# Layer 1 starts its queries and keys on half of the width, with its opening loads in another order

## The chip, the core and the metric

One core of a Trainium2 chip runs the kernel. The time is that of the device, in microseconds (us), from the first to the last instruction of one execution and what lies around it. Five engines work in parallel, each through its own list of instructions in order: PE (matmul; PEld is its weight load), DVE and POOL (elementwise), ACT (activations, and a queue of DMAs), SP (only DMAs).

## The reference

Two layers of a hybrid transformer run over 512 latent tokens (x) and 256 context tokens (ctx), width 1024, in fp32. The change touches the first lines of a layer: modulation, norm, and the queries and keys of the neighbourhood attention.

```python
mod = (jax.nn.silu(c) @ mod_w[i] + mod_b[i])[:, None, :]
mod_c = (jax.nn.silu(c_ctx) @ mod_w[i] + mod_b[i])[None, None, :]
sh_m, sc_m, g_m, sh_f, sc_f, g_f = jnp.split(mod, 6, axis=-1)
csh_m, csc_m, cg_m, csh_f, csc_f, cg_f = jnp.split(mod_c, 6, axis=-1)
h = rms_norm(x, norm_attn_w[i]) * (1.0 + sc_m) + sh_m
hc = rms_norm(cx, norm_attn_w[i]) * (1.0 + csc_m) + csh_m
ua, ub, ug = jnp.split(h @ w_in[i], splits, axis=-1)
uca, ucb, ucg = jnp.split(hc @ w_in[i], splits, axis=-1)
ya, yca = neighbourhood_attention(ua, uca, na_rpb[i], ctx_out)
yb, ycb = ssd_mixer(ub, ucb, ...)
yg, ycg = gqa_attention(ug, ucg, ...)
x = x + g_m * (jnp.concatenate([ya, yb, yg], axis=-1) @ w_out[i])
# then a SwiGLU with sh_f, sc_f, g_f, the same for ctx in layer 1 only, and a last rms_norm
```

## The kernel before

The width of 1024 is cut into eight slices of 128 (d or k = 0 to 7) on the partitions; a row of a tile is a slice over 768 tokens, 512 of x and 256 of ctx. An fp32 product is made of three matmuls of rounded parts (high by high, low by high, high by low). load_w (L332) loads a weight block of 128x1024 into wr, ACT copies the high part into wh (L336), and DVE takes the low part wl as the difference (L337). make_h (L314) makes the normed and modulated activations: a multiply by the token scale and by the modulation scale on DVE or ACT and POOL (L324 to L327), the high part by ACT with the shift as bias (L329), the low part by DVE (L330). The high parts are HY for d 0 to 3 and HS for d 4 to 7, the low parts HZ and PHA, PHB.

The modulation of a layer has 12 chunks of 512 columns. In layer 1 chunk 0 and 1 are the two halves of the shift, 2 and 3 those of the scale; one half serves d 0 to 3, the other d 4 to 7. mod_chunk (L187) computes one on PE from eight loads of 256 KB (L179): eight matmuls with 32 columns of weights (L189), a copy to SBUF on DVE (L196), small transposing matmuls (L199), the sum with the bias (L201) and, for a scale, L265. Chunks 4 to 9 are made aside while the projections run: mod_rows (L207) loads the two conditioning vectors as rows (in_cvec, through the MA and MB buffers, L213) and takes their SiLU (L214 to L216), and mod_dots multiplies rows of the transposed weights by them on POOL (L239), sums on ACT (L240) and ends in two adds on DVE (L248, L250). The program's generator md spreads these over the stages.

The opening loads x by token blocks, then chunks 0 and 2, ctx, and chunks 1 and 3 (SP queue); blocks 0 and 1 of w_blk (queries of the neighbourhood attention) come behind. With all four chunks and both scales there, make_h runs for x and ctx, and the 192 matmuls of blocks 0 and 1 (L348) run over d = 0 to 7. spill (L541, on ACT's DMA queue) sends the queries to DRAM through MA and MB, two buffers each. Then come blocks 2 and 3 (keys, each spilled as it is done), the weights of the grouped attention's keys and values (w_kvdt, L362), and blocks 4 and 5 (values, transposed at L595). S is a PSUM tile of 128x1024, of which there are two; PT and sm are half as large, two each. Later stages of layer 1, in order: head_out with the rotary step on DVE (L678 on POOL, L694 and L697 on DVE), the convolution (L771), the remaining projections, attention (scores L400) and the state-space chunks, whose decay row goes through DRAM (crow, L876 and L901). skip (L937) multiplies on POOL.

A scheduler orders the instructions of each engine from the code's priorities and a simulated timeline; so what a diff moves in the code is not what moves on each engine.

## Time and profile before

| what | value |
|---|---|
| median of three runs | 1828.59 us |
| lowest and highest | 1812.85 and 1829.15 us |
| the profiled execution | 1826.39 us |
| its span, first to last instruction | 1824.6 us |
| mean granted clock of TensorE | 0.976 |
| busy of the span: PE, PEld, DVE, ACT, POOL | 95%, 81%, 58%, 37%, 22% |
| HBM traffic | 121 GB/s over the span |

The profile is of one execution. Times in it are from the start of the span. A line of a timeline gives start and duration of a run of like instructions, and in brackets how long the engine sat idle before it and what ended that.

### The profile page before, as it was taken

What the parts mean: (1) busy time and instruction counts of PE and PEld (TensorE: products, weight loads), DVE (VectorE), ACT (ScalarE), POOL (GpSimd) and SP (SyncE); (2) the same over time, 40 slices, a digit from 0 to 9 for tenths busy, and PEclk for the clock granted to TensorE, in tenths of its full rate; (3) what the DMA queues carried; (4) which work ended last, traced back from release to release, by engine and by line L of the source; (5) the groups of instructions that cost most, each with busy time, mean ns of one, the idle gap of its engine ahead of it and who ended that gap; (6) DMA issues with size and microseconds to landing.
All of it is one profiled execution on the core that took longest, in us unless ns stands there. A gap on an engine that the chain in (4) does not pass through costs nothing.

```text
span 1824.6 us, 26613 instructions
## 1 busy us (share of the span) xinstructions
PE 1735.0 (95%) x10146; PEld 1477.7 (81%) x10146; DVE 1056.2 (58%) x2165; ACT 683.9 (37%) x1376; POOL 401.6 (22%) x429
## 2 busy tenths in 40 slices
...
GB/s 364 186 152 123 194 144 182 122 89 66 73 61 135 119 116 117 114 103 118 115 127 115 120 157 189 81 114 112 150 74 65 98 93 93 104 94 94 102 106 79
DMA packets 94319, 221.66 MB, mean 121 GB/s; under 512 B 18416, under 2 KB 26224, under 8 KB 94192
## 3 DMA queue, kind: packets, MB, share of 16 engines
...
q14 instruction: 47, 0.39, 0.1%
HBM read 198.49 MB, written 21.43 MB: 121 GB/s over the span
## 4 chain that ended last, share of the span: by engine, by line
PE 78%; DVE 8%; DMA 6%; ACT 3%; issue 3%; POOL 2%; SPq 0%; ACTq 0%; DVEq 0%; POOLq 0%
PE S L348 60%; DMA wl<-crow 3%; PE sm L446 3%; PE PT L362 2%; PE sm L362 2%; PE PT L434 2%; DMA wr<-in_mod_wT_dram 1%; PE S L400 1%; PE PT L348 1%; PE sm L930 1%; PE sm L931 1%; PE PT L975 1%; PE S L189 1%; PE S L403 1%; DVE wl L337 1%
## 5 line engine op out<-in xcount | busy, mean ns | idle before, releaser
L336 ACT ACTIVATE wh<-wr 128x1024 fp32r<-128x1024 f32 (+3 forms) x204 | 197.9, 971 | 721.0 <-PE S L348 534.7
L337 DVE TENSOR_TENSOR wl<-wr,wh 128x1024 fp32r<-128x1024 f32 (+3 forms) x204 | 231.0, 1133 | 176.1 <-ACT wh L336 173.8
L280 POOL TENSOR_TENSOR tiny<-tiny,mhalf 128x2 f32<-128x2 f32 (+2 forms) x17 | 28.7, 1689 | 1068.3 <-DVE tiny L1181 1019.8
L348 PE MATMUL S<-HY,wh 128*128 128x512 f32 (+1 forms) x716 | 217.0, 361 | 8.8 <-DVE MB L294 4.5
L348 PE MATMUL S<-HZ,wh 128*128 128x512 f32 (+1 forms) x716 | 213.8, 356 | 0.6 <-DVE HZ L330 0.6
L348 PE MATMUL S<-HY,wl 128*128 128x512 f32 (+1 forms) x716 | 212.1, 354 | 0.7 <-DVE wl L337 0.7
L348 PE MATMUL S<-HS,wh 128*128 128x512 f32 (+1 forms) x716 | 212.3, 354 | 0.0
L348 PE MATMUL S<-HS,wl 128*128 128x512 f32 (+1 forms) x716 | 209.1, 350 | 0.0
L242 DVE CUSTOM_DVE_ANT_0 PT<-wr,XFB 128x512 f32<-128x512 f32 x112 | 75.6, 716 | 185.8 <-DMA wr<-in_mod_wT_dram 185.8
L348 PEld LDWEIGHTS S<-HY,wh 128*128 128x128 f32 x716 | 119.4, 192 | 27.3 <-issue 4.7
L348 PEld LDWEIGHTS S<-HZ,wh 128*128 128x128 f32 x716 | 120.0, 192 | 22.4 <-DVE HZ L330 2.1
L348 PEld LDWEIGHTS S<-HY,wl 128*128 128x128 f32 x716 | 118.3, 191 | 20.1 <-DVE wl L337 1.0
L348 PEld LDWEIGHTS S<-HS,wh 128*128 128x128 f32 x716 | 117.2, 189 | 18.2
L348 PEld LDWEIGHTS S<-HS,wl 128*128 128x128 f32 x716 | 116.2, 188 | 18.9
L348 PE MATMUL S<-PHA,wh 128*128 128x512 f32 (+1 forms) x358 | 105.8, 352 | 0.0
L348 PE MATMUL S<-PHB,wh 128*128 128x512 f32 (+1 forms) x358 | 104.6, 350 | 0.0
L348 PE MATMUL S<-GX,wh 128*128 128x512 f32 (+1 forms) x400 | 97.7, 350 | 0.4 <-DVE KA L1135 0.4
L425 POOL TENSOR_SCALAR pr<-pr,tiny 128x640 f32<-128x640 f32 (+2 forms) x80 | 68.1, 854 | 99.7 <-DVE tiny L424 78.6
L434 PE MATMUL PT<-c,pr 128*128 128x128 f32 x384 | 67.2, 292 | 11.1 <-ACT PHA L438 3.6
L1282 DVE TENSOR_TENSOR MB<-S,MA 128x768 f32<-128x768 f32 (+1 forms) x42 | 34.6, 824 | 70.5 <-PE S L348 70.5
L239 POOL TENSOR_TENSOR KA<-QN,XFB 128x512 f32<-128x512 f32 x48 | 67.1, 1404 | 36.9 <-ACT XFB L216 24.5
L348 PEld LDWEIGHTS S<-GX,wh 128*128 128x128 f32 x400 | 65.9, 189 | 11.2 <-DVE KA L1135 0.8
...
## 6 DMA issues: line engine op xcount, KB each, us to landing
...
```

The lines of the kernel that those rows point to most:

```text
L189: PE.matmul(pm[32 * j : 32 * j + 32, 0:512], lhsT=cs[:, k, :], rhs=w[k], start=(k < 4), stop=(k >= 4), tile_position=(0, 32 * j),)
L239: G.tensor_tensor(out=p_, in0=wv, in1=x, op=ALU.mult)
L242: V.tensor_tensor_reduce(out=p_, in0=wv, in1=x, scale=1.0, scalar=0.0, op0=ALU.mult, op1=ALU.add, accum_out=acc[:, o : o + 1],)
L280: POW.tensor_tensor(out=y, in0=v, in1=mhalf[:, 0:n], op=ALU.pow)
L336: S.activation(hi, raw, AF.Copy)
L337: V.tensor_tensor(lo, raw, hi.bitcast(F32), ALU.subtract)
L348: ins = PE.matmul(pt[:, c0:c1], lhsT=w, rhs=xx[:, c0:c1], start=(k == (0 if len(order) == 1 else order[0]) and i == 0), stop=(k == (nk - 1 ...
L362: PE.matmul(pt[:, 0:n], lhsT=s, rhs=w[:, o : o + n], start=(k == 0 and i == 0), stop=(k == KB - 1 and i == 2),)
L425: G.tensor_scalar(out=p_, in0=p_, scalar1=m[:, 4:5], scalar2=1.0, op0=ALU.mult, op1=ALU.mult)
L434: PE.transpose(pt[:, k * P : (k + 1) * P], pr[j, qi][:, kk * P : (kk + 1) * P], ident)
L446: PE.matmul(pv[64 * j : 64 * j + 64, 0:P], lhsT=V2(kts[k], j), rhs=ph[j, qi][:, k, :], start=(k == 0), stop=(k == nkt - 1), tile_position= ...
L1282: V.tensor_tensor(gg[:, c0:c1], pu[:, c0:c1], sg[:, c0:c1], ALU.mult)
```

## The change

The opening of layer 1 is written anew. All of x is loaded first (half of it into other buffers, so that the loads do not wait for MA and MB), then chunks 0 and 2, and the token scale of x is made at once. Behind chunk 2 come blocks 0 and 1 of w_blk, chunk 1, ctx, blocks 2 and 3 (their raw tiles in the wh and wl buffers, their parts in vh and vl), and chunk 3. make_h runs for d 0 to 3 of x with chunks 0 and 2 alone. near(0) multiplies blocks 0 and 1, near(2) blocks 2 and 3, over those four slices of x: two S tiles hold four results of 512 columns. After chunk 3 the other four slices follow, and then all eight over ctx into PT tiles; class Two presents S and PT as one result. All four results are spilled before mod_rows (before: the two queries were, and the keys behind it). Blocks 4 and 5 are loaded ahead of w_kvdt, in both layers. Layer 2 is otherwise as it was. The constants are loaded in two parts.

```diff
...
@@ -150,13 +150,18 @@
+        def rest():
+            nc.scalar.dma_start(c1[:, NEAR:ncol], a["cpk1"][:, NEAR:ncol])
+            nc.scalar.dma_start(c2, a["crow"].to_broadcast([P, nrow]))
...
@@ -326,12 +330,16 @@
-            S.activation(hi, t1, AF.Identity, bias=sh)
-            V.scalar_tensor_tensor(lo, t1, sh, hi.bitcast(F32), ALU.add, ALU.subtract)
-
-    def load_w(src, n, to="w"):
-        raw = T(sb, "wr", 2, [P, n])
-        nc.sync.dma_start(raw, src)
+            ia = S.activation(hi, t1, AF.Identity, bias=sh)
+            iv = V.scalar_tensor_tensor(lo, t1, sh, hi.bitcast(F32), ALU.add, ALU.subtract)
+        return ia.ins, iv.ins
+
+    dma = [None]
+
+    def load_w(src, n, to="w", raw=None):
+        if raw is None:
+            raw = T(sb, "wr", 2, [P, n])
+        dma[0] = nc.sync.dma_start(raw, src).ins
...
@@ -463,7 +471,7 @@
-            xin = (ma if hf == 0 else mb)([P, 512])
+            xin = slot("HZ" if tb in (2, 3) else "GT" if tb == 4 else "GC")[:, 0:512] if tb > 1 else (ma, mb)[hf]([P, 512])
...
@@ -487,18 +495,16 @@
-    mod_chunk(0, 0, mw[0])
-    mod_chunk(0, 2, mw[1])
-    for tb in range(4, 6):
-        load_tok(tb)
-    mw = [mod_loads(0, 1, ["wh", "wl", "XFB", "XFB", "YO", "HD"]), mod_loads(0, 3, HT[4:8] + HT[12:16])]
-    for c0, c1 in ((0, 4), (4, 6)):
+
+    def token_scale(c0, c1):
-    mod_chunk(0, 1, mw[0])
-    mod_chunk(0, 3, mw[1])
+
+    token_scale(0, 4)
+    mod_chunk(0, 0, mw[0], ps_s())
+    mod_chunk(0, 2, mw[1], ps_s())
...
@@ -542,17 +542,75 @@
                 r.append(d)
             return r
 
-        ws = [wblk(i) for i in range(2)]
-        pts = [ps_s(), Split()]
-        for seg in osegs:
-            for k in range(KB):
-                for w, pt in zip(ws, pts):
-                    proj_ws(pt, w[0], w[1], hh, hl, KB, [seg], [k])
+        xsp = []
+
+        class Two:
+
+
+            def __init__(self, x, c):
+                self.t = x, c
+
+            def __getitem__(self, idx):
+                c0, c1 = idx[1].start, idx[1].stop
+                return self.t[0][:, c0:c1] if c0 < 512 else self.t[1][:, c0 - 512 : c1 - 512]
+
+        if last:
+            hh, hl = h_tiles()
+            sc1 = scale_tiles(l, 1, naw[l])
+            for r_, part in zip(rstd, xcp):
+                make_h(l, xT, (hh, hl), r_, part, 0, sc1)
+            ws = [wblk(i) for i in range(2)]
+            pts = [ps_s(), Split()]
+            for seg in osegs:
+                for k in range(KB):
+                    for w, pt in zip(ws, pts):
+                        proj_ws(pt, w[0], w[1], hh, hl, KB, [seg], [k])
+        else:
+            ws = [wblk(i) for i in range(2)]
+            with tc.issue_after(dma[0]):
+                mw = [mod_loads(0, 1, GT[0:8])]
+            ws += [wblk(i, "v", T(sb, t, WB[t], [P, 1024])) for i, t in ((2, "wh"), (3, "wl"))]
+            with tc.issue_after(dma[0]):
+                mw.append(mod_loads(0, 3, HT[4:8] + HT[12:16]))
+            hh, hl = h_tiles()
+            sc1 = scale_tiles(l, 1, naw[l], (0,))
+            make_h(l, xT, (hh, hl), rstd[0], xcp[0], 0, sc1, range(4))
+            pxs = [ps_s() for _ in range(2)]
+            pts = [pxs[i // 2][:, 512 * (i % 2) : 512 * (i % 2) + 512] for i in range(4)]
+
+            def near(i):
+                for k in range(4):
+                    for w, pt in zip(ws[i : i + 2], pts[i : i + 2]):
+                        ins = proj_ws(pt, w[0], w[1], hh, hl, KB, xsegs, [k])
+                return ins
+
+            with tc.issue_after(near(0)):
+                ins = near(2)
+                mod_chunk(0, 1, mw[0], ps_sm())
+            with tc.issue_after(ins):
+                mod_chunk(0, 3, mw[1], ps_sm())
+                for tb in range(4, 6):
+                    load_tok(tb)
+            sc1 += scale_tiles(l, 1, naw[l], (1,))
+            make_h(l, xT, (hh, hl), rstd[0], xcp[0], 0, sc1, range(4, KB))
+            with tc.issue_after(ins):
+                token_scale(4, 6)
+            ia, iv = make_h(l, xT, (hh, hl), rstd[1], xcp[1], 0, sc1)
+            load_rest()
+            for w, pt in zip(ws, pts):
+                for k in range(4, KB):
+                    proj_ws(pt, w[0], w[1], hh, hl, KB, xsegs, [k])
+            pcs = [ps_t() for _ in range(2)]
+            pts = [Two(pts[i], pcs[i // 2][:, 256 * (i % 2) : 256 * (i % 2) + 256]) for i in range(4)]
+            for w, pt in zip(ws, pts):
+                proj_ws(pt, w[0], w[1], hh, hl, KB, asegs[1:])
         for d in range(KB):
             t = dr.tile([P, NT], F32, name=nm("xsp"), tag=f"xsp{l}_{d}")
             nc.sync.dma_start(t[:, 0:ntok], xT[d][:, 0:ntok])
             xsp.append(t)
         nqk = [spill(pts[i], ntok, "nq", 0.125, True) for i in range(2)]
+        if not last:
+            nqk += [spill(pts[i], ntok, "nk", 1.0, True) for i in range(2, 4)]
         md = iter(())
         if not last:
             rows = mod_rows()
...
@@ -566,11 +624,18 @@
         step_md = lambda n: [next(md, None) for _ in range(n)]
         for i in range(2, 4):
             step_md(4)
+            if not last:
+                continue
             w = wblk(i)
             pt = ps_s()
             proj_ws(pt, w[0], w[1], hh, hl, KB, asegs)
             nqk.append(spill(pt, NT, "nk", 1.0, True))
 
+        with ExitStack() as es:
+            if not last:
+                es.enter_context(tc.issue_after(ia))
+                es.enter_context(tc.issue_after(iv))
+            wv = [wblk(4 + b) for b in range(2)]
         wkv = []
         for i in range(3):
             k0, k1 = 3 * i, min(3 * i + 3, 8)
             step_md(4)
-            w = wblk(4 + b)
+            w = wv[b]
             pt = ps_s()
             proj_ws(pt, w[0], w[1], hh, hl, KB, asegs)
             t = mb([P, NT])
```

On SP, behind the last load of chunk 2 (mod_w into GR), the order before reads as follows; XFB, YO and HD hold chunk 1, HS and PHA and PHB chunk 3, MA and MB blocks of ctx.

```order
25 L179 DMA GR_212<-in_mod_w_dram 128x512
26 L179 DMA wh_314<-in_mod_w_dram 128x2x512
27 L179 DMA wl_316<-in_mod_w_dram 128x2x512
28 L179 DMA XFB_318<-in_mod_w_dram 128x512
...
42 L179 DMA PHB_338<-in_mod_w_dram 128x512
43 L179 DMA PHB_340<-in_mod_w_dram 128x512
44 L334 DMA wr_503<-in_w_blk_dram 128x1024
45 L334 DMA wr_509<-in_w_blk_dram 128x1024
46 L553 DMA xsp_614<-KA_77 128x768
```

In the changed kernel the same place, where GV to GB hold chunk 1 (rows 28 to 35) and HS to PHB chunk 3 (rows 42 to 49), reads:

```order
25 L184 DMA GR_212<-in_mod_w_dram 128x512
26 L342 DMA wr_273<-in_w_blk_dram 128x1024
27 L342 DMA wr_279<-in_w_blk_dram 128x1024
28 L184 DMA GV_285<-in_mod_w_dram 128x512
...
39 L475 DMA GC_489<-in_ctx_dram 128x512
40 L342 DMA wh_301<-in_w_blk_dram 128x1024
41 L342 DMA wl_307<-in_w_blk_dram 128x1024
42 L184 DMA HS_313<-in_mod_w_dram 128x512
...
49 L184 DMA PHB_327<-in_mod_w_dram 128x512
50 L342 DMA wr_928<-in_w_blk_dram 128x1024
51 L342 DMA wr_934<-in_w_blk_dram 128x1024
```

Two weight blocks moved ahead of chunk 1, two more ahead of chunk 3, and the values' blocks 4 and 5 to right behind it.

On ACT, around the spills and the SiLU of the conditioning rows, the order before has the queries' four spill DMAs and then the first row (wh is a weight split, S_515, PT and sm hold the queries):

```order
78 L336 ACTIVATE wh_938<-wr_936 128x544
79 L541 DMA nq_636<-MA_630 128x768
80 L541 DMA nq_648<-MB_641 128x768
81 L541 DMA nq_638<-MB_631 128x768
82 L336 ACTIVATE wh_1004<-wr_1002 128x1024
83 L214 ACTIVATE XFB_650<-MA_651 128x512
84 L216 ACTIVATE XFB_650<-XFB_650 128x512
```

In the changed kernel, from the last query spill on (S_365 and PT_631 hold the keys):

```order
82 L541 DMA nq_762<-MB_755 128x768
83 L297 ACTIVATE MA_764<-S_365 128x512
84 L344 ACTIVATE vh_948<-wr_946 128x816
85 L297 ACTIVATE MA_764<-PT_631 128x256
86 L541 DMA nk_770<-MA_764 128x768
87 L297 ACTIVATE MA_774<-S_365 128x512
88 L541 DMA nk_772<-MB_765 128x768
89 L297 ACTIVATE MA_774<-PT_631 128x256
90 L344 ACTIVATE wh_954<-wr_952 128x544
91 L541 DMA nk_780<-MA_774 128x768
92 L541 DMA nk_782<-MB_775 128x768
93 L344 ACTIVATE wh_1497<-wr_1495 128x1024
```

The four key spills moved ahead of the rows: the first L218 (L214 before) is row 94 now.

On POOL, around the fourth multiply of raw keys (GR by c), the order before is this; L239 rows are the multiplies for modulation chunks, 28 of which stand ahead of row 48:

```order
43 L239 TENSOR_TENSOR QN_821<-QN_821,HD_668 128x512
44 L239 TENSOR_TENSOR KA_837<-QN_835,XFB_656 128x512
45 L678 TENSOR_TENSOR GR_1206<-GR_1206,c_216 128x128
46 L239 TENSOR_TENSOR QN_828<-QN_828,YO_662 128x512
47 L239 TENSOR_TENSOR KA_844<-QN_842,XFB_650 128x512
48 L678 TENSOR_TENSOR GR_1206<-GR_1206,c_216 128x128
```

In the changed kernel, with L243 for L239 and L743 for L678:

```order
29 L743 TENSOR_TENSOR GR_1210<-GR_1210,c_216 128x128
30 L243 TENSOR_TENSOR QN_844<-QN_844,HD_802 128x512
31 L243 TENSOR_TENSOR KA_860<-QN_858,XFB_790 128x512
32 L743 TENSOR_TENSOR GR_1210<-GR_1210,c_216 128x128
33 L243 TENSOR_TENSOR QN_851<-QN_851,YO_796 128x512
```

The fourth multiply moved from behind 28 of the chunk rows to behind 14. At the end of these rows on POOL the changed kernel has, where the 96 stood ahead of every L937 before (L1002 is that skip multiply now):

```order
138 L243 TENSOR_TENSOR QN_1547<-QN_1547,HD_802 128x512
139 L1002 TENSOR_TENSOR HY_2927<-GX_1215,c_216 128x256 x3
140 L1002 TENSOR_TENSOR HY_2929<-GX_1217,c_216 128x256 x3
141 L243 TENSOR_TENSOR KA_1596<-QN_1594,XFB_790 128x512
142 L1002 TENSOR_TENSOR HY_2926<-GX_1214,c_216 128x256 x3
143 L1002 TENSOR_TENSOR HY_2928<-GX_1216,c_216 128x256 x2
144 L243 TENSOR_TENSOR QN_1587<-QN_1587,YO_796 128x512
...
148 L243 TENSOR_TENSOR QN_1594<-QN_1594,HD_802 128x512
```

Three of the 96 moved behind skip multiplies.

## Rows read from the trace of the kernel before

**Rows 1.** The page: busy time of each engine and its share of the span.

```profile
PE 1735.0 (95%) x10146; PEld 1477.7 (81%) x10146; DVE 1056.2 (58%) x2165; ACT 683.9 (37%) x1376; POOL 401.6 (22%) x429
```

**Rows 2.** Stretches: us, busy per engine (instructions), granted clock, DMA share, GB/s.

```profile
20.00:30.00 10.00, 8.60 (x50) 3.56 (x50) 2.95 (x14) 2.89 (x11) 1.02 (x1) 1.00 1.05 387
...
90.00:100.00 10.00, 10.00 (x49) 8.64 (x48) 0.42 (x1) 4.85 (x15) 9.48 (x10) 0.81 1.00 311
...
160.00:170.00 10.00, 10.00 (x72) 9.35 (x72) 9.89 (x15) 4.68 (x9) 9.80 (x4) 1.00 0.56 169
```

**Rows 3.** Timeline of PE: start, duration, operation, idle time before, its releaser.

```profile
22.55 1.81 PE L189 MATMUL S<-GR,cs 128*32 128x512 f32 x5
...
37.30 1.66 PE L189 MATMUL S<-PHB,cs 128*32 128x512 f32 x4
...
41.87 0.50 PE L348 MATMUL S<-HY,wh 128*128 128x512 f32 x1 [0.33 <-ACT wh L336]
...
49.84 0.39 PE L348 MATMUL S<-HS,wh 128*128 128x512 f32 x1
...
79.00 0.28 PE L362 MATMUL sm<-vl,HY 128*128 128x272 f32 x1
...
88.82 0.98 PE L348 MATMUL S<-HY,wh 128*128 128x512 f32 x2 [4.51 <-DVE MB L294]
...
99.59 0.52 PE L348 MATMUL S<-HY,wh 128*128 128x512 f32 x2
...
269.77 0.42 PE L400 MATMUL S<-KA,QN 128*128 128x384 f32 x1
...
1090.27 0.66 PE L348 MATMUL S<-HY,wh 128*128 128x512 f32 x1 [1.49 <-ACT HY L329]
```

**Rows 4.** Timeline of DVE, the opening and the first of line 694.

```profile
27.06 0.17 DVE L265 SCALAR_TENSOR_TENSOR sc<-mod,c 128x8 f32<-128x8 f32 x1
...
37.06 2.43 DVE L327 SCALAR_TENSOR_TENSOR MA<-KA,sc,pr 128x512 f32<-128x512 f32 x2 [0.20 <-ACT pr L311]
...
40.36 0.73 DVE L330 SCALAR_TENSOR_TENSOR HZ<-MA,mod,HY 128x512 fp32r<-128x512 f32 x1
...
43.22 2.34 DVE L337 TENSOR_TENSOR wl<-wr,wh 128x1024 fp32r<-128x1024 f32 x2
...
45.49 0.15 DVE L265 SCALAR_TENSOR_TENSOR sc<-mod,c 128x8 f32<-128x8 f32 x1
...
124.79 7.59 DVE L694 TENSOR_TENSOR pr<-GR,c 128x64 f32<-128x64 f32 x1 [0.31 <-POOL GR L678]
```

**Rows 5.** Chain of work that ended last, in order of time: start, duration, what.

```profile
68.43 5.22 DMA nq<-MA
...
73.70 5.77 DMA MA<-in_cvec_dram
...
219.83 3.04 PE PT L362 x24
...
234.64 8.33 PE S L348 x48
...
274.63 7.20 DMA wl<-crow
```

**Rows 6.** Timeline of POOL, from the first steady multiplies to the skips.

```profile
84.31 1.27 POOL L239 TENSOR_TENSOR QN<-QN,YO 128x512 f32<-128x512 f32 x1 [1.41 <-DMA MB<-in_cvec_dram]
...
124.30 0.46 POOL L678 TENSOR_TENSOR GR<-GR,c 128x128 f32<-128x128 f32 x1
...
160.20 7.06 POOL L280 TENSOR_TENSOR tiny<-tiny,mhalf 128x36 f32<-128x36 f32 x1 [0.98 <-DVE tiny L275]
...
258.85 1.33 POOL L239 TENSOR_TENSOR QN<-QN,HD 128x512 f32<-128x512 f32 x1
...
270.92 3.48 POOL L937 TENSOR_TENSOR HY<-GX,c 128x256 f32<-128x256 f32 x6 [10.74 <-PE sm L362]
```

**Rows 7.** Waits, 125 to 290 us: waiter, releaser, total us, times, longest.

```profile
POOL KA L239 <- ACT KA L240: 6.5, 2, 4.1
```

40 lines of the change are left out of this document (17 added, 23 removed).

## The prediction

> **What bounds it now.** The page gives PE 95% of the span [rows 1], so time comes off only where PE waits or runs at a low clock. I read PE's waits first, then the table of stretches, then the chain of work back from each wait. In layer 1 the first waits lie in the opening 112 us, the only ones that the change aims at. Up to 40 us the DMA engines are the limit: their share is 1.05 at 387 GB/s [rows 2], so 512 KB take 524 KB / 387 GB/s = 1.35 us and 256 KB 0.68 us. PE has little but chunk matmuls then. Its last ones for chunk 2 run from 22.55 to 24.36, those for chunk 3 begin to end at 37.30, and the first projection starts at 41.87 [rows 3]. The scale of chunk 2 is there at 27.06 and lies unused for 15 us; that of chunk 3 comes at 45.49, behind two weight splits of 1.17 us on DVE [rows 4]. The first matmul on the far half of the width is at 49.84 [rows 3].
>
> Queries and keys are done when block 3 ends at 79.00 [rows 3]. After some key/value matmuls PE sits 4.51 us for the evacuation of the key blocks and starts block 4 at 88.82 [rows 3]. The granted clock was 0.81 in 90 to 100 us [rows 2]: block 4 took 99.59 - 88.82 = 10.77 us [rows 3], where a block at full clock takes 8.33 for its 48 matmuls [rows 5]. These are 24 pairs of 512 and 256 columns, 0.347 a pair: 0.23 and 0.12 us.
>
> After that DVE is the busiest beside PE (9.89 of 10 us in 160 to 170 [rows 2]). POOL meanwhile multiplies rows for modulation chunks 4 to 9 (I call one such instruction a dot): 96 dots of 1.3 us, steady from 84.31, the last ending at 258.85 + 1.33 = 260.18 [rows 6].
>
> **Part by part.**
>
> *Loads.* No byte is added. Blocks 0 and 1 of the weights come right behind chunk 2, blocks 2 and 3 ahead of chunk 3: four loads of 1.35 us, so chunk 3 lands 5.4 us later, near 37.3 + 5.4 = 42.7. Blocks 0 and 1 land near 25.3; blocks 2 and 3, behind chunk 1 and the context, near 22.55 + 4 x 1.35 + 12 x 0.68 = 36.1. In the order the rest of the constants is issued early all the same, so splitting their load costs and gains nothing.
>
> *Near half.* First matmul at 27.06 + 1.2 (multiply) + 0.7 (ACT, taken like DVE's 0.74 for one such tile) = 29, instead of 41.87. The 24 matmuls of blocks 0 and 1 are 24 x 0.23 = 5.5 us, but DVE needs about 9 to supply them (three multiplies of 1.22, four low parts of 0.74, two splits of 1.17 [rows 4]); they end near 37. Blocks 2 and 3 are split by 39.5, and their 24 matmuls end at 45 (at half clock, with twice the price, at 50).
>
> *Far half.* Chunk 3's matmuls now stand on PE behind these. From the end of chunk 2's to its scale it took 27.06 - 24.36 = 2.7 us; chunk 3 needs 1.66 [rows 3] for its own, so the scale comes at 49.5 and the first far matmul at 51.5. Bounds: 49.6 (the landing decides) and 56 (near half at half clock). Then 48 x 0.23 = 11, about 1 for a slow start, and 96 context matmuls of 0.12 = 11.5: queries and keys end at 75. Gain 4.0, bounds 0 and 6.
>
> *Blocks 4 and 5.* Their weights load at the end of the opening, and the S tiles of the far half can be evacuated while PE does the context columns. So the 4.51 us wait goes, and 10.77 - 8.33 = 2.4 us of slow clock with it. PE comes to the work behind block 5 about 4.0 + 4.5 + 2.4 = 10.9 us earlier; bounds 7 and 13. Late next is POOL.
>
> [...]
>
> *Modulation rows.* All four spills now precede the loads of the conditioning rows, which share the MA and MB buffers. Before, the first of these loads went out when a query spill had landed (68.43 + 5.22) and took 5.77 [rows 5]; the dots ran steadily from 84.31. After, it waits for the first key spill, which on ACT stands behind a split that needs block 3's weight buffer (75): spill at 77.5, landed 83, row loaded 89, steady dots from about 91. That is 7 us later (bounds 4 and 11). But fewer dots stand ahead of the main work on POOL: before, 28 ahead of the fourth weight multiply of the raw keys, at 124.30, for which DVE's line 694 waits at 124.79 [rows 4, 6]; after, 14. So it is possible at 91 + 14 x 1.3 + 5 x 0.46 = 111.5, 12.8 earlier: POOL does not hold the main chain there, and the 10.9 can pass to DVE's long stretch.
>
> *Where it comes back.* The dots that were put behind must still end before attention gets its last buffers. Ahead of the 7.06 us instruction at 160.20 [rows 6] stand 27 dots, before 42. With the chain it moves to about 149.5 and ends at 156.6; 69 dots of 1.3 are 89.7, and other work and waits on POOL were 260.18 - 167.26 - 54 x 1.3 = 22.7. If all of these stay, POOL ends at 269; if they shrink to 9, at 255. Attention's first score ran at 269.77 [rows 3], after the dots; what it needs in earnest, the decay row, is loaded from 274.63 to 281.83 [rows 5], and that comes about 10 earlier. POOL in the middle, 262, would then cost 2 to 3 of the 10.9. I take 2.6.
>
> *Layer 2.* The code there moves two weight loads ahead and key/value matmuls back. Before, 24 of them, 3.04 / 24 = 0.13 us each [rows 5], filled in behind waits as that of 1.49 at 1090.27 [rows 3]. Not to have them there costs 0 to 3 us; I take 1.5.
>
> **Sum.** 10.9 - 2.6 - 1.5 = 6.8 us. The profiled execution took 1826.39 (span 1824.6, so 1.8 around it), against a median of 1828.59 over 1812.85 to 1829.15. 1826.4 - 6.8 = 1819.6, say 1820. A measurement of this kernel tells about 1% (18 us) from no change; all idle time of PE in the stretch touched is less.
>
> **Rivals.**
> - *All of it arrives:* POOL ends by 256 and layer 2 loses nothing: 1826.4 - 10.9 = 1815.5. For it: the 22.7 us hold waits for the main chain, 6.5 us on ACT's line 240 alone [rows 7], which go if the chain is earlier. Chance 0.25.
> - *Slower: the dots hold attention.* The last three dots now stand behind the skip multiplies, which wait for the end of PE's projections (10.74 us before, until 270.92 [rows 6]). This decides if POOL's other dots end past 272 and a buffer of the first query and key set hangs on the last three. With the late bound for the first dot (95) and no wait saved they end at 273; three dots and 9 us of skips make 286, 16 later than 269.77, of which PE's remaining projections and z matmuls fill about 8 and the earlier chain 3: 1826.4 + 5 = 1831. Against it: in the order the first set's buffers come free before the skips. Chance 0.15.
> - *Hidden anyway:* DVE's stretch is paced by something that does not move, as the dot chain; then only layer 2 counts: 1826 to 1828. Against it: 14 dots instead of 28 ahead. Chance 0.15.
> - My forecast, part of the gain arrives (1817 to 1823): chance 0.45.
>
> **Range.** From 1808 (all of it, and half of the 16 us between the runs shown) to 1831. The likeliest case's own is 1815 to 1825. Faster by over 1% needs 18 us, more than every microsecond named: 0.06, mostly the spread of the runs. Slower by over 1%: 0.05. Within: 0.89.
>
> **What would show it.** First projection near 29 us; a pause of PE from 46 to 51; queries and keys done near 75; no wait ahead of block 4 and the clock there at 1.00; steady dots from about 91, DVE's work on line 694 from about 114; the 7.06 us instruction near 150; POOL's last dot between 255 and 269; attention's first scores 3 to 8 us earlier. I am wrong if chunk 3 lands after 46, if the fourth multiply on POOL comes after 120, or if layer 2 opens more than 3 us longer.

## The result, and the profile after

The changed kernel is slower: a median of 1842.78 us (1841.93 to 1846.46, four runs) beside 1826.46 for the kernel before on the same chip, a ratio of 1.0093 with a 95% interval from 1.0064 to 1.0121. The forecast was 1820, with a range from 1808 to 1831. The profiled execution has a span of 1841.2 us (before 1824.6), so 16.6 us are to be found.

Engine work is the same, as the page's busy times show beside [rows 1]:

```profile
PE 1735.3 (94%) x10146; PEld 1480.2 (80%) x10146; DVE 1057.5 (57%) x2165; ACT 684.4 (37%) x1376; POOL 397.8 (22%) x429
```

So PE waits 16 us longer. The stretches of the changed kernel (columns as in [rows 2]) show two places, the opening and the 30 us ahead of attention:

```profile
20.00:30.00 10.00, 6.45 (x36) 2.77 (x30) 3.31 (x9) 2.80 (x4) 0.53 (x1) 0.82 1.05 398
30.00:40.00 10.00, 6.68 (x15) 4.92 (x16) 8.36 (x10) 5.12 (x7) 1.71 (x1) 0.50 1.05 392
...
50.00:60.00 10.00, 6.68 (x49) 4.19 (x48) 5.80 (x17) 6.75 (x21) 3.21 (x3) 0.85 0.44 171
...
90.00:100.00 10.00, 10.00 (x58) 8.64 (x57) 2.82 (x4) 2.98 (x5) 0.89 (x1) 1.00 0.93 322
...
270.00:280.00 10.00, 4.02 (x30) 3.55 (x28) 5.55 (x11) 8.86 (x25) 8.51 (x8) 0.78 0.61 198
280.00:290.00 10.00, 2.50 (x8) 2.10 (x8) 5.15 (x17) 3.20 (x7) 10.00 (x16) 0.50 0.88 251
290.00:300.00 10.00, 3.54 (x13) 3.17 (x13) 7.76 (x19) 5.89 (x18) 5.12 (x6) 0.50 0.95 248
```

From 270 to 300 PE is busy 4.02 + 2.50 + 3.54 = 10.1 us, at a granted clock of 0.78 and then twice 0.50. The kernel before had 5.95, 4.61 and 9.34 there, 19.9 us:

```profile
270.00:280.00 10.00, 5.95 (x39) 5.12 (x37) 8.21 (x22) 2.54 (x6) 9.08 (x16) 0.90 0.66 166
280.00:290.00 10.00, 4.61 (x17) 3.84 (x18) 7.71 (x23) 6.58 (x19) 3.62 (x5) 0.50 0.73 252
290.00:300.00 10.00, 9.34 (x52) 6.61 (x52) 7.28 (x20) 5.85 (x14) 5.72 (x7) 0.74 0.12 39
```

From 270 to 380 PE is busy for 79.7 us now and was for 90.9 before, 11.2 us less in the same time. The timeline of PE in the changed kernel, as [rows 3]:

```profile
31.00 0.79 PE L356 MATMUL S<-HY,wh 128*128 128x512 f32 x1 [2.83 <-ACT HY L333]
...
49.77 0.95 PE L203 MATMUL sm<-c,SA 128*128 128x2 f32 x8
50.64 1.07 PE L193 MATMUL sm<-HS,cs 128*32 128x512 f32 x8
...
58.79 0.79 PE L356 MATMUL S<-HS,wh 128*128 128x512 f32 x1 [3.06 <-ACT HS L333]
...
84.50 0.52 PE L356 MATMUL S<-HY,wh 128*128 128x512 f32 x2
...
110.76 0.39 PE L370 MATMUL PT<-vh,HY 128*128 128x272 f32 x1 [0.47 <-DVE GV L661]
...
283.70 0.69 PE L408 MATMUL S<-KA,QN 128*128 128x384 f32 x1 [4.98 <-DMA KA<-nk]
...
294.76 0.66 PE L408 MATMUL S<-KA,QN 128*128 128x384 f32 x1 [8.57 <-DMA wl<-crow]
...
454.58 0.97 PE L356 MATMUL S<-GR,wh 128*128 128x512 f32 x4
```

Two rows of the kernel before, to compare with those at 110.76 and 454.58:

```profile
112.02 0.39 PE L362 MATMUL PT<-vh,HY 128*128 128x272 f32 x1 [0.97 <-DVE GV L596]
...
436.93 0.96 PE L348 MATMUL S<-GR,wh 128*128 128x512 f32 x4
```

The near half starts at 31.00 instead of 41.87, but the far half at 58.79 instead of 49.84; block 4 follows at 84.50 without a wait (before 88.82, behind 4.51 of waiting). The key/value matmuls behind the value transposes, by which time PE has done the same work in both kernels, run at 110.76 instead of 112.02. The whole new opening is worth 1.3 us there. Attention's first scores then come at 283.70 instead of 269.77, and the next ones wait 8.57 us more.

POOL, as [rows 6], and the queue of loads on SP (the first row is five loads, with the time from the first to the last issue):

```profile
103.42 2.54 POOL L243 TENSOR_TENSOR KA<-QN,XFB 128x512 f32<-128x512 f32 x2 [3.02 <-ACT XFB L220]
...
156.11 7.71 POOL L284 TENSOR_TENSOR tiny<-tiny,mhalf 128x36 f32<-128x36 f32 x1
...
266.24 1.29 POOL L243 TENSOR_TENSOR QN<-QN,YO 128x512 f32<-128x512 f32 x1
270.10 1.30 POOL L243 TENSOR_TENSOR KA<-QN,XFB 128x512 f32<-128x512 f32 x1 [2.56 <-ACT KA L244]
...
279.01 3.47 POOL L1002 TENSOR_TENSOR HY<-GX,c 128x256 f32<-128x256 f32 x6
...
289.45 1.27 POOL L243 TENSOR_TENSOR QN<-QN,HD 128x512 f32<-128x512 f32 x1
```

```profile
260.81 13.75 SPq L236 DMA_DIRECT2D QN<-in_mod_wT_dram  x5
...
278.89 1.18 SPq L376 DMA_DIRECT2D KA<-nk  x2
...
290.96 0.33 SPq L966 DMA_DIRECT2D wl<-crow  x1
```

The dots run steadily from 103.42 (before 84.31) and end at 289.45 + 1.27 = 290.7 (before 260.18), the last three among the skips of line 1002. The loads of the last dots' weights keep the queue from 260.81 to 274.56. Attention's keys are issued behind them and behind the store of the decay row (at 276.81), at 278.89, and the decay row is loaded at 285.18 to 290.96; before, the row began to load by 274.63 [rows 5]. So the first score does not wait for the last dot itself, which ends 7 us after it, but for loads that stand behind those of the dots. Pieces of the chain that ended last, on the way to that score, as in [rows 5]:

```profile
261.46 6.09 DVE tiny L252
...
271.40 2.50 DMA QN<-in_mod_wT_dram
274.04 1.28 POOL KA L243
...
279.49 4.17 DMA KA<-nk
```

The first piece is an instruction held on DVE; a section below is about it. Behind the first scores little more is lost: the first matmul of the output projection on tile GR runs at 454.58 (before 436.93, so 17.6 later), and the end of the span is 16.6 later.

### The profile page after: what moved, and what is told of

The parts are those of the page before. It is cut to its first block, busy times and chain, and to the rows that moved or that the text cites. A ratio compares the mean times of both kernels' runs of the same rounds, so it can differ in the third digit from the quotient of the medians.

```text
span 1841.2 us, 26624 instructions
## 1 busy us (share of the span) xinstructions
PE 1735.3 (94%) x10146; PEld 1480.2 (80%) x10146; DVE 1057.5 (57%) x2165; ACT 684.4 (37%) x1376; POOL 397.8 (22%) x429
## 4 chain that ended last, share of the span: by engine, by line
PE 75%; DVE 8%; DMA 7%; POOL 3%; issue 3%; ACT 3%; SPq 0%; ACTq 0%; DVEq 0%; POOLq 0%
PE S L356 59%; PE sm L454 3%; DMA wl<-crow 3%; PE PT L442 2%; PE PT L356 1%; PE PT L370 1%; PE S L408 1%; DMA wr<-in_mod_wT_dram 1%; POOL KA L243 1%; PE sm L370 1%; POOL QN L243 1%; PE sm L995 1%; PE sm L996 1%; PE S L411 1%; DVE wl L345 1%
## 5 line engine op out<-in xcount | busy, mean ns | idle before, releaser
L356 PE MATMUL S<-HY,wh 128*128 128x512 f32 (+1 forms) x700 | 213.3, 362 | 6.8 <-ACT HY L333 6.8
L433 POOL TENSOR_SCALAR pr<-pr,tiny 128x640 f32<-128x640 f32 (+2 forms) x80 | 68.0, 854 | 99.4 <-DVE tiny L432 79.2
L243 POOL TENSOR_TENSOR KA<-QN,XFB 128x512 f32<-128x512 f32 x48 | 66.1, 1381 | 46.4 <-ACT XFB L220 29.4
```

The lines of the kernel that those rows point to most:

```text
L243: G.tensor_tensor(out=p_, in0=wv, in1=x, op=ALU.mult)
L356: ins = PE.matmul(pt[:, c0:c1], lhsT=w, rhs=xx[:, c0:c1], start=(k == (0 if len(order) == 1 else order[0]) and i == 0), stop=(k == (nk - 1 ...
L433: G.tensor_scalar(out=p_, in0=p_, scalar1=m[:, 4:5], scalar2=1.0, op0=ALU.mult, op1=ALU.mult)
```

## The experiments

All runs are lined up by one number: that first matmul on GR, given as its distance from 436.93 of the kernel before. It is read from one execution of each, and it need not go with the time: e8 is 12.2 us late there and only 6.8 at the end of its span (1831.4 us). Start and end of the dots, the decays (PE's first matmuls on dA, line 860 before and 925 in the changed kernel: the end of the main chain of work ahead of attention) and the first score are from each run's profile; the ratio is that of the timed runs to those of the kernel before on the same chip, with its 95% interval.

| kernel | dots from | to | decays | first score | GR matmul | ratio |
|---|---|---|---|---|---|---|
| before | 81.6 | 260.2 | 268.3 | 269.8 | 0 | 1 |
| changed | 99.1 | 290.7 | 268.7 | 283.7 | +17.6 | 1.0093 (1.0064 to 1.0121) |
| e1 | 91.9 | 272.7 | 269.0 | 273.3 | +2.1 | 0.9997 (0.9981 to 1.0014) |
| e2 | 92.4 | 271.5 | 269.5 | 271.6 | +9.6 | 1.0039 (1.0005 to 1.0073) |
| e3 | 87.1 | 274.8 | 288.8 | 290.3 | +24.4 | 1.0127 (1.0110 to 1.0144) |
| e5, 64 dots | 99.2 | 236.0 | 267.5 | 268.9 | +2.6 | 1.0027 (1.0008 to 1.0045) |
| e6, 64 dots | 82.6 | 204.1 | 264.8 | 266.2 | -0.5 | 1.0018 (1.0004 to 1.0033) |
| e7 | 103.4 | 293.4 | 269.4 | 301.8 | +22.9 | 1.0100 (1.0023 to 1.0177) |
| e8 | 85.4 | 270.7 | 277.3 | 278.7 | +12.2 | 1.0017 (0.9995 to 1.0040) |
| e9 | 88.0 | 269.9 | 278.6 | 280.1 | +15.5 | 1.0053 (1.0023 to 1.0083) |
| e10 | 97.8 | 279.9 | 264.2 | 283.2 | +17.9 | 1.0102 (1.0063 to 1.0141) |
| e11 | 83.1 | 271.7 | 275.8 | 277.3 | +10.2 | 1.0048 (1.0027 to 1.0069) |
| e12 | 92.6 | 282.8 | 281.9 | 284.1 | +17.9 | 1.0072 (1.0050 to 1.0094) |
| e13 | 98.8 | 289.2 | 275.3 | 290.3 | +20.0 | 1.0051 (1.0028 to 1.0075) |
| e14, 80 dots | 99.2 | 256.2 | 266.1 | 267.5 | +3.5 | 1.0018 (1.0007 to 1.0030) |
| e15, 112 dots | 82.4 | 296.3 | 274.8 | 304.1 | +21.9 | 1.0120 (1.0094 to 1.0145) |
| e16 | 99.4 | 287.8 | 262.9 | 296.3 | +20.8 | 1.0104 (1.0072 to 1.0135) |
| e17 | 98.0 | 237.0 | 265.7 | 267.1 | +2.2 | 1.0211 (1.0181 to 1.0241) |
| e19 | 101.2 | 260.2 | 267.2 | 268.6 | +2.4 | 1.0093 (1.0061 to 1.0125) |
| e20 | 82.5 | 236.8 | 266.4 | 267.8 | +0.7 | 1.0128 (1.0086 to 1.0169) |

### When the rows of the dots are loaded: e1, e2, e3, e8

e1 is the kernel before with the loads of the conditioning rows put behind all four spills, as the change does:

```diff
         md = iter(())
+        for i in range(2, 4):
+            w = wblk(i)
+            pt = ps_s()
+            proj_ws(pt, w[0], w[1], hh, hl, KB, asegs)
+            nqk.append(spill(pt, NT, "nk", 1.0, True))
+
         if not last:
             rows = mod_rows()
 ...
-        for i in range(2, 4):
+        for _ in range(2 if not last else 0):
             step_md(4)
-            w = wblk(i)
 ...
-            nqk.append(spill(pt, NT, "nk", 1.0, True))
```

> The kernel before, with one thing of the change alone: the conditioning rows are made behind all four spills of queries and keys, not between the queries' and the keys' spills. The opening stays that of before. Theory A (the late start of the POOL multiplies for chunks 4 to 9, the dots, is the loss): the first dot starts near 96 us instead of 81.6, steady dots near 100 instead of 84.3, the last dot ends 12 to 17 us later than 260.2, attention's first query and key loads go out behind it, and the kernel takes 1834 to 1843. Theory B (the loss comes from the half-width start itself, from the order of projections it leaves on PE, or from the order around attention in the changed kernel): the time stays within 1823 to 1829.

Measured: no difference in time (0.9997). The dots ended 12.5 us later, at 272.7, and the first score came 3.6 later. The loss that the changed kernel has did not appear, so a later start of the dots alone, by 10 us, is not what costs 16; an end at 272.7 is still nearly free.

e2 is the changed kernel with the rows between the query and the key spills:

```diff
-            nqk += [spill(pts[i], ntok, "nk", 1.0, True) for i in range(2, 4)]
 ...
             step_md(4)
+            nqk.append(spill(pts[i], ntok, "nk", 1.0, True))
```

> The changed kernel with the conditioning rows made between the queries' and the keys' spills, as the kernel before has them. What the first runs left: attention starts at the later of two things, the main chain (PE's projections, whose end stayed at 268 to 269 us in three kernels) and the last dot; a last dot at 272.7 cost nothing, one at 290.7 cost 17. Theory A (two gates): the first dot comes about 6 us earlier than 99.1, the last one ends at 280 to 285, and the time is 1826 plus 7 to 12, so 1833 to 1838. Theory B (the dots do not decide, the order around attention in the changed kernel does): 1840 to 1845.

Measured: the dots end at 271.5, 19 us earlier than in the changed kernel, and the first score comes at 271.6, 12 earlier. A wait of 2.88 us ahead of block 4 is back. The GR matmul is 9.6 late and not 17.6. Half of the loss goes. The fourth score was still only 1.1 late (285.06, before 283.96), the ninth 7.1 (321.18, before 314.10): the other half is lost inside attention, and its cause is open. The time, 9.0 us over the kernel before, is what theory A expected, but not for its reason: the dots ended at 271.5 and not at 280 to 285.

e3 and e8 load the rows in place, without MA and MB, so that no spill holds them: e3 right behind the loads of chunk 3, e8 behind all of make_h.

```diff
-            nc.sync.dma_start(x, a["cvec"][...].to_broadcast([P, 512]))
+            nc.sync.dma_start(t, src)
+            S.activation(x, t, AF.Tanh, scale=0.5)
 ...
+                rows = mod_rows(True)          # e3: behind mod_loads(0, 3, ...)
+            with tc.issue_after(ia), tc.issue_after(iv):
+                rows = mod_rows(True)          # e8: behind make_h
```

> The changed kernel, with one thing undone in another way: the four conditioning rows are loaded behind chunk 3 straight into their own tiles, with MA and MB only as scratch, so that they wait for no spill. Theory A: dots start when the x slices in the QN buffers have been stored, near 66 to 70 us instead of 99; the last one ends before 260, attention's loads go out before PE's projections end, and the kernel takes 1819 to 1829 (13 to 24 less than 1842.8). Theory B: dots start early as well, but the time stays within 1838 to 1845.

> The changed kernel with the rows loaded early into their own tiles as in the earlier run, but their arithmetic put behind the normed activations, so that ACT does not wait for them ahead of the half-width start (that wait of 22 us on PE is what the earlier run paid). Theory A (two gates): the first dot near 76 to 82, the last before 265, PE's projections end as in the changed kernel (dA near 268 to 269), time 1823 to 1829. Theory B: 1838 to 1845.

e3 is slower still (1.0127). PE's timeline tells why: on ACT the tanh of the rows now stands ahead of the near half's tiles and waits for its load, and PE waits for ACT.

```profile
50.81 0.79 PE L364 MATMUL S<-HY,wh 128*128 128x512 f32 x1 [22.25 <-ACT HY L341]
```

Twenty microseconds lost in the opening arrive whole at the decays (288.8) and at the GR matmul (+24.4). In e8 the opening is unhurt and the dots run from 85.4, but the decays come at 277.3, 8.6 late, and its root on POOL (the 7.06 us instruction of [rows 6]) at 167.65 (changed 156.11), behind 41 dots (changed 27). So there is a second gate: dots that begin early stand ahead of the main chain's work on POOL and delay the decays. In time e8 is the only kernel with the new opening and all 96 dots in front that is not clearly slower (1.0017, from 0.9995); 1823 to 1829 us were expected and 1835.66 came, beside 1831.44.

### Fewer dots and more: e5, e6, e14, e15

These change the dots' number. e5 (changed kernel) and e6 (kernel before) leave out chunks 8 and 9, whose place chunks 6 and 7 take; e14 (changed kernel) leaves out chunk 9, for which chunk 7 stands; e15 (kernel before) computes chunk 9 twice.

```diff
-                for c in range(4, 10)
+                for c in range(4, 8)                 # e5, e6: 64 dots
+                for c in range(4, 9)                 # e14: 80 dots
+                for c in (4, 5, 6, 7, 8, 9, 9)       # e15: 112 dots
```

> The changed kernel without modulation chunks 8 and 9 (a scale's two halves for the second half of the layer; chunks 6 and 7 stand in their place), so 64 dots instead of 96, from the same late start. Theory A: the last dot ends near 289 - 32 x 1.3 - 6 = 241 to 250, attention's loads go out before 260, and the kernel takes 1820 to 1830. Theory B: 1838 to 1845.

> Control for the run with 64 dots: the kernel before without chunks 8 and 9 in the same way. Theory A says that in the kernel before the dots end in time (260 against a first score at 269.8), so leaving a third of them out saves at most 4 us: 1820 to 1828. If it saves more than 8, the kernel before was held by its dots too and the run with 64 dots shows less than it seems.

> The changed kernel without the 16 dots of modulation chunk 9 (chunk 7's result stands in for it), so 80 dots instead of 96; with 64 the matmul on which all runs can be lined up (output projection, 436.93 in the kernel before) came 2.6 us later than before, with 96 it came 17.6 later. Theory G (two gates: what counts is when the dots end, and nothing is lost while they end before about 272): 16 dots and the wait among the last of them are about 24 us, so they end at 263 to 268, first score 268 to 272, that matmul 2 to 6 us later than before, time within 5 us of the run with 64 (about 4 us over the kernel before). Theory P (the number of dots that share POOL and hold DVE is what costs, in proportion): halfway, 10 us later than before, and a time 9 us over the kernel before.

> The kernel before with the 16 dots of chunk 9 done twice (112 dots), nothing else. Theory G: the dots, which ended at 260.18, end at 281 to 287, about where those of the changed kernel do (290.72); the first score moves from 269.77 to 277 to 283 and the aligning matmul of the output projection from 436.93 to 444 to 452, the time 6 to 14 us over the kernel before, though the opening is untouched. Theory O (the changed kernel is slower for something in its new opening or in its loads, and the dots only stand by): no more than 3 us over the kernel before.

In the changed kernel 64 dots give +2.6 at the GR matmul, 80 give +3.5 and 96 give +17.6. That is no cost in proportion to their number: the first 16 of those 32 dots cost 1 us and the last 16 cost 14. The 80th ends, and the first score follows the decays at once:

```profile
254.87 1.32 POOL L243 TENSOR_TENSOR QN<-QN,HD 128x512 f32<-128x512 f32 x1
```

```profile
267.49 0.42 PE L408 MATMUL S<-KA,QN 128*128 128x384 f32 x1
```

e15 makes the loss appear in the kernel before, whose opening is untouched: +21.9, ratio 1.0120, more than the 6 to 14 us expected. The rows of its POOL, of the first score on PE, and of DVE:

```profile
285.58 1.27 POOL L239 TENSOR_TENSOR KA<-QN,XFB 128x512 f32<-128x512 f32 x1 [2.94 <-ACT KA L240]
...
295.03 1.27 POOL L239 TENSOR_TENSOR QN<-QN,HD 128x512 f32<-128x512 f32 x1
```

```profile
304.06 0.66 PE L400 MATMUL S<-KA,QN 128*128 128x384 f32 x1 [15.90 <-DMA KA<-nk]
```

```profile
267.76 14.90 DVE L248 TENSOR_TENSOR tiny<-tiny 128x8 f32<-128x8 f32 x1
```

PE waits 15.90 us for keys. Their load goes out at 296.78, behind the store and the loads of the decay row on the same queue, and the store waited for ACT, which stood behind the DVE addition of 14.90 us:

```profile
SPq L876 <- ACT SA L869: 8.5, 1, 8.5
```

e5, e14 and e15 together show that dots which still run when attention is due are the cause: take the last of them away and the loss goes, add as many to the other kernel and it comes. They do not show by which of two ways it comes, as loads that stand behind the dots' on the queue or as DVE held while POOL multiplies. All seven profiles with a last dot at 279.9 or later have a small DVE instruction held for 4.95 to 16.85 us, beginning between 258 and 268; no profile with an earlier end has one there. Against the hold alone speaks that its length does not go with the loss: 4.95 us in e10 with +17.9, 16.82 in e16 with +20.8. A run with late dots and no hold is missing. In the profile of e15 the main chain was 6.5 us late too (decays 274.8), behind one wait of 7.06 for a dot's weights at 228, so not all of the 21.9 is the last dots'. e6 shows that the kernel before gains nothing certain from fewer dots (1.0018): its 260.2 lay below the gate.

### The additions that end a chunk: e13, e10, e12, e11

The trace of DVE in the changed kernel has one odd row, an addition of 128 x 8 numbers just ahead of the convolution steps of line 836:

```profile
261.38 6.17 DVE L252 TENSOR_TENSOR tiny<-tiny 128x8 f32<-128x8 f32 x1
267.48 1.01 DVE L836 SCALAR_TENSOR_TENSOR MB<-S,c,MB 128x771 f32<-128x771 f32 x1
```

In this section, held means that an instruction took far longer than its form takes elsewhere. The same form took 0.15 us at 261.35 in the kernel before. The changed kernel's waits name what follows, ACT's dot copies waiting for DVE:

```profile
ACT KA L244 <- DVE SA L878: 6.7, 2, 6.0
...
POOL KA L243 <- DMA QN<-in_mod_wT_dram: 6.4, 2, 5.0
```

e13 puts the skips and first weighings behind the last dot; e10 does that and computes the additions on POOL between two dots; e12 is e2 with the additions on POOL, e11 the kernel before with them.

```diff
+                with tc.issue_after(dot[0]):      # e13, e10: dot[0] is the last dot
                     xe = weigh(i, dd)
+            with tc.issue_after(dot[0]):
                 skip(c)
 ...
-        V.tensor_tensor(acc[:, 0:8], acc[:, 0:8], acc[:, 8:16], ALU.add)
+        G.tensor_tensor(acc[:, 0:8], acc[:, 0:8], acc[:, 8:16], ALU.add)   # e10, e11, e12
```

> The changed kernel, with one thing altered: on POOL the skip multiplies (line 1002 of the changed kernel) and the first weighings (line 1021) are put behind the last dot. In the changed kernel the last three dots lie between them: the 93rd dot ends at 279.05, the 96th at 290.72, and the decay row is only loaded at 285.18 to 290.96. Theory G (two gates ahead of the first score: the dots' end and the main chain): the dots end near 284 (three times 1.3 and one wait for a row load of about 1.4), the first score is at 276 to 279 instead of 283.70, and the time is 4 to 8 us less, 1835 to 1839. Theory M (the main chain alone sets it; the three dots stand in work that waits for PE anyway): the first score moves, but the time stays at 1841 to 1845.

> As the run with the dots ahead of the skips, and besides the two small additions that end a modulation chunk (lines 252 and 254 of the changed kernel, 128 x 8) run on POOL between two dots instead of on DVE. In the changed kernel the one at 261.38 took 6.17 us on DVE, until POOL paused, where the same form took 0.15 elsewhere. Theory P (a DVE instruction with two inputs from SBUF is held while POOL streams, and ACT and then the dots themselves wait for DVE): DVE's convolution step at 267.48 comes at 261.5, the 2.56 us pause of POOL at 270.10 goes, the decays on PE (268.69 in the changed kernel) come at 261 to 264, the dots end near 280, first score 272 to 276, time 1828 to 1835. Theory Q (the 6 us are put down wrongly, or the chain waits for something else there): the decays stay at 267 to 270 and the time is that of the run with the dots ahead of the skips alone, within 2 us.

> The changed kernel with the conditioning rows loaded between the query and the key spills (as in the run e2, dots from 92.4 to 271.5, time 1840.43 there beside 1831.44 of the kernel before) and with the small additions on POOL. In e2 one of them was held on DVE for 4.68 us at 121.93 and one for 4.16 at 253.32. Theory P: the decays on PE come at 260 to 264 instead of 269.54, the dots end by 268, the first score is at 264 to 268, and the time is 4 to 7 us under that of the kernel before, 1820 to 1824: it beats both. Theory Q: decays at 268 to 271, first score at 270 to 273, time that of the kernel before, within 4 us.

> Control: the kernel before with the small additions on POOL and nothing else. There none of them was held on DVE for more than 1.27 us, so theory P and theory Q both expect the time of the kernel before within 3 us and the decays on PE within 2 us of 268.32; a gain of more than 4 us would say that the additions cost something else than the hold.

e13: 1837.73 beside 1827.64, 10 us over the kernel before instead of 16, where 4 to 8 us less than the changed kernel were expected. The intervals of the two ratios overlap slightly, so this supports the gate without settling it. Its profiled execution is the longest of those timed, has a wait of POOL of 7.09 us ahead of 229.11 that the profile of the changed kernel lacks, and an addition held for 6.21 us at 267.78, so its row of the table shows nothing of the 5 us.

e10: no addition is held, but the next DVE instruction of the same size is, the scale made from the sum (line 283; lines 281 in e12 and 277 in e11). So the hold was moved and not taken away:

```profile
266.28 4.95 DVE L283 SCALAR_TENSOR_TENSOR sc<-mod,c 128x8 f32<-128x8 f32 x1 [4.10 <-POOL mod L263]
```

The decays come at 264.20, 4.5 earlier than in the changed kernel. That says nothing of the hold: 3.5 of it is there before (PE's transposes of GR at 212.79 instead of 216.28), and in the changed kernel PE is busy without a break from 250 to 270, so its decays did not wait for the addition at 261. What waited was ACT, and behind it the dots and the store of the decay row. The first score does not move in e10, and the time does not fall:

```profile
264.20 1.03 PE L939 MATMUL sm<-dA,c 128*128 128x96 f32 x8
...
283.23 0.66 PE L422 MATMUL S<-KA,QN 128*128 128x384 f32 x1 [7.64 <-DMA KA<-nk]
```

The dots end at 279.9 as expected. The keys' load goes out at 279.20, as soon as ACT has summed a dot in the buffer that they need (278.46 + 0.72 = 279.18); ACT was late with it behind DVE, so here both ways meet. 272 to 276 was expected for the score; the loads behind the dots were left out of that sum, and the hold on the scale was not foreseen. e11 and e12 are slower than what they were made from, which neither theory had. Their dots end at 271.7 instead of 260.2 and at 282.8 instead of 271.5. The additions take 0.40 and 0.20 us in the mean on POOL in e11, but the scale behind them is held on DVE for 7.41 us at 266.45 in e12 and in e11, where the kernel before had no hold at this place, for 7.53:

```profile
251.95 7.53 DVE L277 SCALAR_TENSOR_TENSOR sc<-mod,c 128x8 f32<-128x8 f32 x1 [0.18 <-POOL mod L257]
```

ACT then waits 7.21 us for DVE and POOL 5.25 for ACT. That is a part of the loss: from 125 to 290 POOL sits idle ahead of the dots into KA for 21.4 us in e11 (11.2 in the kernel before) and 20.3 in e12 (11.3 in e2), for ACT and for loads, and where the rest of it comes from is open. What the changed kernel would take without any hold none of the runs shows.

### The opening: e7, e9, e16

e7 puts chunks 1 and 3 ahead of the second half of the near matmuls and the context behind the far half's tiles; e9 does so with the rows early, as e8; e16 only puts the context's evacuations behind the far half's tiles.

```diff
             with tc.issue_after(near(0)):
-                ins = near(2)
                 mod_chunk(0, 1, mw[0], ps_sm())
                 mod_chunk(0, 3, mw[1], ps_sm())
+                ins = near(2)                                     # e7, e9
+            iq, ir = make_h(l, xT, (hh, hl), rstd[0], xcp[0], 0, sc1, range(4, KB))
+            with tc.issue_after(ins), tc.issue_after(iq), tc.issue_after(ir):   # e16
                 for tb in range(4, 6):
                     load_tok(tb)
```

> The changed kernel with chunk 3's matmuls and the far half's activations ahead of the second near half and of the context blocks in the code, the step that my sum had wrong (first far matmul at 58.8 instead of 51.5). Theory A: the first far matmul comes at 50 to 54, queries and keys are done at 76 to 80 instead of 84.8, PE's projections end 5 to 8 us earlier (dA at 261 to 264), but the dots still start behind the spills (near 93) and end near 282 to 287: 1832 to 1839. Theory C (what the opening gains passes to the end whatever the dots do): 1834 to 1838 with the first score as much earlier as dA, that is near 277.

> Both edits together: far half first, and rows early behind the activations. Theory A (two gates): dA at 261 to 264, last dot before 263, and time 1818 to 1824, 3 to 9 less than the kernel before. If the time stays at 1826 to 1830 though dA is earlier, there is a third gate at attention's start that I have not named.

> The changed kernel with the evacuation of the context tokens on ACT and DVE put behind the tiles of the far half (before it, six evacuations of 0.3 to 0.6 us each lay on ACT and four on DVE between the scale of chunk 3 at 55.13 and the first far matmul at 58.79). Theory C (these evacuations and not the scale hold the far half): first far matmul at 56.5 to 57.3, but the context columns come later by as much, so queries and keys end at 84 to 87 as in the changed kernel (84.8), and the time is that of the changed kernel within 3 us. Theory S (the scale holds it): first far matmul at 58 to 59, same time.

In e7 the far half began at 60.73 and in e9 at 64.57, no earlier than 58.79. Chunk 3 ahead of the near matmuls does not help, and the time shows no gain either (1.0100 and 1.0053). In e16 PE's far half begins 1.1 us earlier. The scale in the changed kernel, then the scale and the first far matmul in e16:

```profile
55.13 0.16 DVE L269 SCALAR_TENSOR_TENSOR sc<-mod,c 128x8 f32<-128x8 f32 x1
```

```profile
54.13 0.17 DVE L269 SCALAR_TENSOR_TENSOR sc<-mod,c 128x8 f32<-128x8 f32 x1
```

```profile
57.69 0.50 PE L356 MATMUL S<-HS,wh 128*128 128x512 f32 x1 [2.88 <-ACT HS L333]
```

From the scale to the matmul it takes 3.56 us in e16 and 3.66 in the changed kernel. So the context's evacuations did not hold the far half, and theory C fails, though the matmul nearly comes when it said. e16's scale is 1.0 earlier since its near half ended at 48.85 (49.77), with a granted clock of 0.66 and not 0.50 in 30 to 40, before anything that the edit touches. The 3.6 us are the way of the first far slice through three engines: a multiply on ACT, one on POOL, and the high part on ACT (L328, L329, L333), which is done 3.5 us behind the scale in e16. Later DVE holds an addition again:

```profile
258.39 16.82 DVE L252 TENSOR_TENSOR tiny<-tiny 128x8 f32<-128x8 f32 x1 [0.56 <-ACT QN L244]
```

The decays came at 262.92, 5.8 earlier than in the changed kernel, but the addition was held 16.82 us, the dots ended at 287.8, and the GR matmul came 20.8 late. In e19, which has e16's opening, the decays came at 267.18; so most of the 5.8 is not the opening's.

### A version with both gates open: e19, e17, e20

If 80 dots are nearly free, the 16 of chunk 9 can be made in the output projection, where POOL is idle. e19 does that on e16, e20 on the kernel before, e17 with chunks 8 and 9 on e16.

```diff
-                for c in range(4, 10)
+                for c in range(4, 9)              # e17: range(4, 8)
 ...
         ysh, ysl_ = [yh[k] for k in WK[4:8]], [yl[k] for k in WK[4:8]]
+        md = iter(())
+        if not last:
+            rows = mod_rows()
+            md = (
+                0
+                for c in range(9, 10)             # e17: range(8, 10)
+                for _ in mod_dots(
+                    0, c, rows, lambda: slot("GB")[:, 0:512], True, lambda: slot("GX")[:, 0:512]
+                )
+            )
+        for _ in md:
+            pass
```

> A complete kernel again. The changed kernel with the context's evacuations behind the far half's tiles (as in e16, where the decays on PE came at 262.92 instead of 268.69) and with the 16 dots of chunk 9 moved into the output projection, where POOL is idle between about 460 and 505 us; the sums of that chunk run on POOL. 80 dots stay in front of attention. Theory G (two gates): the early dots end at 250 to 258, the decays stay at 261 to 265, first score 263 to 267, the aligning matmul 1 to 5 us earlier than in the kernel before (436.93); if the 16 late dots end before the norm behind the output projection the time is 1822 to 1828, the same as the kernel before or up to 4 us better; if they do not, 3 to 10 us come back there. Theory P (the dots' number, not their end): as e14, 4 us or more over the kernel before whatever the late dots do.

> As e19, with chunks 8 and 9 moved into the output projection: 64 dots in front of attention, 32 behind it. Theory G: before attention no different from e19 within 2 us, since neither number of dots reaches the gate; but 32 dots of 1.3 us are 42 us in the 45 us that POOL is idle there, behind four loads of the conditioning rows, so the norm behind the output projection waits for them, 5 to 20 us: time 1830 to 1845.

> Control for e19: the kernel before with the 16 dots of chunk 9 moved into the output projection in the same way. Its dots ended before the gate anyway, so theory G expects the first score within 3 us of 269.77 and, apart from what the late dots cost behind the output projection, the time of the kernel before: e20 minus e19 is then what the opening and the context's order are worth, 2 to 6 us.

Up to the output projection the loss is gone: e19 is 2.4 us late at the GR matmul, e17 2.2, e20 0.7, and none of the three has a hold ahead of attention. The gain of 1 to 5 us expected for e19 there did not come: with the dots out of the way the new opening is worth nothing, e19 being 1.7 later than e20. Behind it all three lose more than they could win. The late dots wait for loads that stand behind others on the queue (in e17 the first starts at 515.81), and PE then waits for the norm. The stretch of e17, columns as in [rows 2]:

```profile
520.00:540.00 20.00, 0.00 (x0) 0.00 (x0) 0.00 (x0) 12.03 (x34) 20.00 (x17) 0.50 0.37 118
```

No kernel of this study beats the kernel before.

## Why the prediction was wrong

**The near half** began at 31.00 (predicted 29) and ended at 49.77. That this is the bound of 50, given for half clock, and not the 45 that the sum took, is partly luck. PE waited 2.31 us for DVE's first low part and then ran blocks 0 and 1 at 0.43 us a matmul up to 39.82 and at 0.23 behind it, to 42.32 instead of 37; chunk 1's matmuls, which the sum left out, took PE until 44.17; blocks 2 and 3 took 5.6 us, 0.23 a matmul. The granted clock was 0.82 in 20 to 30, where PE was busy for 6.45 of 10 us, 0.50 in 30 to 40 and 1.00 in 40 to 50. So most of blocks 0 and 1, which the sum priced at 0.23 us a matmul, ran at half clock.

**The far half** is the first failed term: 51.5 predicted with a bound of 56, 58.79 measured. Chunk 3's matmuls could only start at 50.64, behind the near half on PE; from their end to the scale it took the 2.7 us predicted. From the scale to the first far matmul it took 3.7 instead of 2: the sum priced one multiply and one high part, but the first far slice needs two multiplies, on ACT and on POOL (3.6 in e16 too). With the clock at 0.85 and 0.81 from 50 to 70, queries and keys were done at 84.5 and not at 75. The term "gain 4.0" was a loss of 5.5, outside its bounds of 0 and 6.

**Blocks 4 and 5** came as predicted: no wait ahead of block 4, which took 92.98 - 84.50 = 8.48 us, and a clock of 1.00 in 80 to 100. These 6.9 us are what made up for the far half: -5.5 + 4.5 + 2.4 = 1.4, and 1.3 was measured at the value transposes. Predicted was 10.9.

**The modulation rows** failed with the far half. Steady dots were put at 91 (88 to 95) and came at 103.42. Of these 12.4 us 9.5 came with the end of the queries and keys. The rest is the spills': the key spill that frees the row's buffer went out only when a query spill had landed from MB, and took 7.88 us where 5.5 were reckoned. The chain of the changed kernel shows them, as [rows 5] did:

```profile
82.78 6.29 DMA nq<-MB
90.21 7.88 DMA nk<-MB
98.16 6.30 DMA MB<-in_cvec_dram
```

That POOL would not hold the main chain was right in kind (27 dots ahead of the root, as predicted), but the chain was not early: the root ran at 156.11, not 149.5, and line 759 (694 before) on DVE at 123.69, not 114.

**Where it comes back** is the term that decided, priced at 2.6 us. Its sum was root's end + 69 dots + other work and waits, from 255 to 269; the dots ended at 290.7. The 69 dots were right. The root ended 7.2 later (163.8 for 156.6), and other work and waits came to 290.7 - 163.8 - 89.7 = 37.2 us instead of 9 to 22.7. The forecast let waits shrink because the main chain would run ahead; it did not, and POOL's waits for ACT were 8.9 (6.5 in [rows 7]), with 6.4 more for loads. 8.2 of the 37.2 are skips and weighings between the last three dots. The longer of the waits for ACT, 6.3 us, stands elsewhere; the other, of 2.56, is that behind the held addition, which no term had. And an end at 262 was taken as a fault of some microseconds in proportion, where the price goes by steps: an end at 272.7 cost 2.1 at the GR matmul in e1, and all seven kernels whose dots ended at 279.9 or later lost 17.6 or more. Between them it is not clean: e2, with 271.5, lost 9.6, for a reason that is open.

**Layer 2** and all else behind the GR matmul cost nothing: +17.6 there, +16.6 at the end, 1.5 predicted.

**The rival that came nearest** is the slower one, "the dots hold attention". Its conditions were that the other dots end past 272 and that a buffer of the first query and key set hangs on the last three. The first came: the 93rd dot ended at 277.72 + 1.33 = 279.05. The second did not: the first score ran at 283.70, between the 93rd dot and the last. What it met were loads behind the dots' loads and the held addition, which the rival did not have; and with the last three dots ahead of the skips (e13) 10 us stayed. Its chance of 0.15 and its price of 5 us were too low: it credited 8 us of filling by PE and 3 of an earlier chain. PE had neither; it waited 4.98 and 8.57 us, and the granted clock was 0.50 from 280 to 300. Since the range ended at that price, it ended 12 us short.
